# Layer 1: modulation steps between the projections, and the scaled triangles of four heads in one operation

## The chip, the cores and the metric

The kernel runs on one core of a Trainium2 chip. The metric is the device time of one execution in microseconds. A core has five engines with an instruction queue each: TensorE (PE; its weight loads are shown as PEld), VectorE (DVE), ScalarE (ACT), GpSimd (POOL) and SyncE (SP), which here only issues transfers of weights. Each works through its queue in order. Results of TensorE go to PSUM, everything else lies in SBUF.

## The reference, cut to what matters

The program is two networks of two layers each, behind one another, over 256 tokens of width 1024. The change lies in layer 1 of the first. That layer mixes tokens in two ways side by side, a state-space scan (`ssd`) and gated linear attention (`gla`), and six vectors made from `c`, the modulation, scale, shift and gate the layer's activations.

```
m_l = (jax.nn.silu(c) @ mod_w + mod_b)[:, None, :]
sh1_l, sc1_l, g1_l, sh2_l, sc2_l, g2_l = jnp.split(m_l, 6, axis=-1)
p_lat = _ada(x, norm1, sh1_l, sc1_l) @ w_in
...
x = x + g1_l * (o_l.astype(x.dtype) @ w_out)
x = x + g2_l * _sq_relu_mlp(_ada(x, norm2, sh2_l, sc2_l), mlp_w1, mlp_w2)
```

One chunk (128 tokens) of `ssd`, where `lac` is the logarithm of the decay per token and head:

```
cum = jnp.cumsum(lac, axis=1)
lmat = jnp.exp(jnp.where(lower, cum[:, :, None] - cum[:, None, :], -jnp.inf))
cb = jnp.einsum('bign,bjgn->bijg', cc, bc)
y = jnp.einsum('bijgr,bjgrp->bigrp', cb[..., None] * lmat, xdt)
y = y + jnp.einsum('bign,bgrpn->bigrp', cc, h) * jnp.exp(cum)[..., None]
```

## The kernel before, in words

Activations lie with the features on the partitions, 256 tokens of the context and 256 of the sequence in the columns. A large product is made with three matmuls of 32-bit numbers split in two parts: high by high, high by low, low by high (`mm3`, lines L219 to L221). Weights come as a stream of tiles `w` of 128x1024 numbers (0.524 MB), fetched on SP's queue into four buffers (L31). For a projection each half of a `w` is split: ScalarE casts it to `hi` (L44), VectorE subtracts to get `lo` (L45); there are four buffers of each. Once both halves are split, `w` is free. `gemm` makes one projection of 128 outputs from one `w`: 24 matmuls of 256 columns for one side, and 48 (from two fetches of the same weights) for context and sequence.

The modulation (`mod_steps`) needs no split: its tiles `w` are used as they are and become free when TensorE has read them. One step is two tiles with four matmuls of 32x256 each (L150; the trace shows every matmul of this number type as two):

```
        for u in range(16):
            k, o = u % 8, u // 8 * 256
            w = st.raw(16 * g + u)
            for j in range(4):
                nc.tensor.matmul(ps[32 * j : 32 * j + 32, o : o + 256], lhsT=self.cs[:, k, :], rhs=w[:, 256 * j : 256 * j + 256], start=(k == 0), stop=(k == 7))
            if u % 2:
                yield
```

Eight steps make a third of the modulation; layer 1 makes two thirds here, 16 steps, 32 tiles. The results are needed in the output projection and behind it.

PSUM has eight banks: two with the tag `mm` (for projections), two `sc`, four `po`.

The part of `layer1` around the change runs so in the program's text: projections for `gla`; `gla`'s levels (lines L1021 to L1109, many short operations on VectorE, ScalarE and GpSimd with short matmuls into `po`); eight projections (0 to 7) each followed by a convolution (`conv`, four operations L850 on VectorE) and a silu; the output of `gla` (L1129 to L1132); eight more projections `z` and `gs` (24 matmuls each); `ssd`. The first eight are six with 48 matmuls and two with 24. `ssd` first makes states in four rounds (transposes L915 and L927, products L933), then outputs: for two chunks, two directions and two groups of four heads a tile `lt` (a triangle of ones, a head's column of `la` as its scale), two matmuls with it (L975, L977), two exponentials, the products `MT` on GpSimd (L980) and `CE` on VectorE (L981), then the output matmuls (L989, L990). Behind it come the output projection, whose first half needs only `gla`'s result (96 matmuls from tiles `o4` to `o7`), and the memory block.

A scheduler turns this text into the queues: it puts ready work of lower rank where an engine would wait by its own estimate, so rows of several parts are mixed; text that stands earlier has the higher rank. Buffers go out in the order in which transfers and tiles are asked for.

Of the kernel before, what the change touches and what calls it, by code (L numbers as in the profile page):

```python
# [14 lines left out]
ALU = mybir.AluOpType  # L15
AX = mybir.AxisListType
PSUM = bass.MemoryType.PSUM
P = 128
# [57 lines left out]
class Kern:  # L76
# [825 lines left out]
    def ssd(self, pool, xs, bm, cm, z, d4, la, wend, etot, c1, out):  # L902
        nc = self.nc
        tri = lambda n: c1[:, COFF1[n][0] : COFF1[n][0] + COFF1[n][1]]
        TRI, ST = [tri("le"), tri("ge")], [tri("gt"), tri("lt")]
# [6 lines left out]
        for t in range(4):  # L912
# [17 lines left out]
            for d, w in xw.items():  # L930
# [9 lines left out]
                elif t == 1:  # L940
                    h = g(f"H{d}", (P, 8, 64))
# [7 lines left out]
                else:  # L949
                    h = hold[d]  # L950
# [5 lines left out]
        for c in range(2):  # L956
            ps = self.psum("sc")
            for gr in range(2):
                nc.tensor.matmul(ps[:, 128 * gr : 128 * gr + 128], lhsT=bm[gr][:, 256 + 128 * c : 384 + 128 * c],
                                 rhs=cm[gr][:, 128 * c : 128 * c + 128], start=True, stop=True)  # L960
            pair = []
            for d in range(2):
                cb = g("cb", (P, 2, 128), 2)
                nc.vector.tensor_tensor(cb, ps[:, 0:256].rearrange("p (g i) -> p g i", g=2),
                                        TRI[d].unsqueeze(1).broadcast_to([P, 2, 128]), op=ALU.mult)
                MT, CE = g("MT", (P, 8, 128), 2), g("CE", (P, 8, 128), 2)
                pair.append((MT, CE))
                for gr in range(2):
                    hs = slice(4 * gr, 4 * gr + 4)
                    lt = g("lt", (P, 4, 128), 2)  # L970
                    for h in range(4):
                        nc.vector.tensor_scalar(lt[:, h, :], TRI[d], la[:, 2 + c, 8 * d + 4 * gr + h : 8 * d + 4 * gr + h + 1], None, op0=ALU.mult)
                    l2 = lt.rearrange("p h i -> p (h i)")
                    p1 = self.psum("sc")
                    nc.tensor.matmul(p1, lhsT=ST[d], rhs=l2, start=True, stop=True)  # L975
                    p2 = self.psum("sc")
                    nc.tensor.matmul(p2, lhsT=self.C("ones"), rhs=l2, start=True, stop=True)  # L977
                    nc.scalar.activation(MT[:, hs, :], p1.rearrange("p (h i) -> p h i", h=4), AF.Exp)
                    nc.scalar.activation(CE[:, hs, :], p2.rearrange("p (h i) -> p h i", h=4), AF.Exp)
                    nc.gpsimd.tensor_tensor(MT[:, hs, :], MT[:, hs, :], cb[:, gr, :].unsqueeze(1).broadcast_to([P, 4, 128]), op=ALU.mult)  # L980
                    nc.vector.tensor_tensor(CE[:, hs, :], CE[:, hs, :],  # L981
                                            cm[gr][:, 128 * c : 128 * c + 128].unsqueeze(1).broadcast_to([P, 4, 128]), op=ALU.mult)
            for q in range(4):
                po = self.psum("po")
                for h in range(2):
                    o = po[64 * h : 64 * h + 64, 0:128]
                    hh = 2 * q + h
                    for d in range(2):
                        nc.tensor.matmul(o, lhsT=xd[d][c][:, hh, :], rhs=pair[d][0][:, hh, :], start=(d == 0), stop=False)  # L989
                        nc.tensor.matmul(o, lhsT=H[d][c][:, hh, :], rhs=pair[d][1][:, hh, :], start=False, stop=(d == 1))  # L990
                cs = slice(128 * c, 128 * c + 128)
                nc.vector.scalar_tensor_tensor(yt[q][:, cs], xs[q][:, 256 + 128 * c : 384 + 128 * c], self.V("d_skip")[:, q : q + 1], po[:, 0:128],
                                               op0=ALU.mult, op1=ALU.add)
# [140 lines left out]
    def layer1(self, xc, xl, sm, hm, HL):  # L1134

        tc, nc, a = self.tc, self.nc, self.a
# [10 lines left out]
        h = []  # L1147
# [56 lines left out]
        cp = pool("cv", C, "right")  # L1204
        cw, cb = [self.small(self.V(n), ALU.mult, 0.5, tag=n, pool=cp) for n in ("conv_w", "conv_b")]

        def silu(t, last):

            u = cp.tile([P, 512], F32, tag="th", name="th")[:, : t.shape[-1]]
            i = nc.scalar.activation(u, t, AF.Tanh)  # L1210
            self.issue(i, last)
            nc.vector.scalar_tensor_tensor(t, u, 1.0, t, op0=ALU.add, op1=ALU.mult)
            return i

        tanh, mods = [], (x for i in (1, 2) for x in self.mod_steps(1, i, cp, "mm"))
        for i in range(8):
            t = (xs + bm + cm)[i]
            self.conv(cp, self.gemm(st, 72 + 8 * i, *(h if i < 6 else h[1:])), i, t, cw, cb)
            if i == 0:
                for _ in mods:  # L1220
                    pass
            tanh.append(silu(t, last))
        for _ in mods:
            pass
        self.table(tanh)
        for _ in gla:
            pass
        last = self.last
        for i in range(8):
            nc.scalar.mul((z + gs)[i], self.gemm(st, 136 + 8 * i, h[1]), 0.5)  # L1230
        M.close()
        G.close()
        H.close()
        with ExitStack() as B:
            ssd = self.ssd(pool("ssd", B), xs, bm, cm, z, *dts, c1, o[:4])
            next(ssd)
            self.table([silu(t, last) for t in z + gs])
            for _ in ssd:
                pass
# [5 lines left out]
        with ExitStack() as B:  # L1245
            op = pool("os1", B, "right")
            self.w_out(1, [self.split(op, o[i], 256, f"o{i}") for i in range(4, 8)], xl, 0, None, st, 0)
            kv, *_ = self.memory(0, kvp, pool("mem", B, "right"))
        with ExitStack() as B:
            op = pool("os1", B)  # L1250
            HL = ExitStack()
            HL.enter_context(C)
            h, sm, step = self.mlp_enter(1, pool("mh1", HL, "right"), 0)
# [565 lines left out]
```

## Time and profile before

| | us |
|---|---|
| three runs, median | 2041.4 (2037.19 to 2044.7) |
| the profiled execution | 2037.99 |
| its span, first to last instruction | 2036.2 |
| TensorE, VectorE, ScalarE, GpSimd busy | 1914.3, 1417.9, 1160.3, 276.1 |

The profiled execution is one of the program's executions; 1.8 us of its time lie outside the span. All times in microseconds that are given as places, like 1077, count from the span's start. Busy times are sums over an engine's instructions without overlap; the ends of matmuls are modelled, so two matmuls that follow each other in 0.118 us are each shown with about 0.28.

### The profile page before, as it was taken

To read this page: it belongs to the slowest core of one execution; us is meant where nothing else is said; L and a number is where in the kernel's file an instruction comes from. 1 tells how busy PE (TensorE), PEld (TensorE's weight loads), DVE (VectorE), ACT (ScalarE), POOL (GpSimd) and SP (SyncE) were. 2 spreads that over 40 slices of the span, in tenths; PEclk is the share of its full clock that TensorE was granted. 3 is DMA by queue.
4 is the path that set the end of the run, shared out by engine and by line. 5 is a ranking of instruction groups with operands and counts; after the bars stand their busy time and mean duration, and the time that the engine had idled before them with its cause. 6 is when DMAs were issued, how large, how long until landed. Compare 5 with 4: busy or idle time off the path is not lost.

```text
span 2036.2 us, 42319 instructions
## 1 busy us (share of the span) xinstructions
PE 1914.3 (94%) x16330; PEld 1727.5 (85%) x16330; DVE 1417.9 (70%) x2962; ACT 1160.3 (57%) x2527; POOL 276.1 (14%) x407
## 2 busy tenths in 40 slices
PE   5999999889999999999979999999999999989997
PEld 2986668669889998899739779999889998889997
DVE  3775876589767685567588977567776656677664
ACT  3554563465545675566546658476565555565553
POOL 1421110230100000001230210000012201012210
PEclk8999999889999999999989999999999999999999
DMA  8432530624115555765376435555325554324553
GB/s 289 167 134 70 186 125 22 207 94 156 43 38 185 186 194 186 240 215 175 119 237 193 133 108 180 184 187 192 109 84 183 181 186 136 104 83 165 181 183 114
DMA packets 91785, 313.26 MB, mean 154 GB/s; under 512 B 10304, under 2 KB 17728, under 8 KB 91584
## 3 DMA queue, kind: packets, MB, share of 16 engines
q1 hardware_dynamic: 83376, 299.94, 44.5%
q10 hardware_dynamic: 8208, 10.63, 1.6%
q8 instruction: 128, 2.10, 0.4%
q14 instruction: 73, 0.60, 0.1%
HBM read 309.48 MB, written 1.05 MB: 153 GB/s over the span
## 4 chain that ended last, share of the span: by engine, by line
PE 74%; DVE 11%; DMA 5%; ACT 5%; issue 3%; POOL 2%; ACTq 0%; POOLq 0%; DVEq 0%; SPq 0%
PE mm L220 16%; PE mm L219 16%; PE mm L221 16%; PE po L220 3%; PE po L221 3%; PE po L219 3%; DMA w<-in_mlp 2%; DVE lo L45 2%; DMA w<-in_mod 2%; PE sc L528 1%; DMA w<-in_w_in 1%; PE po L1380 1%; PE mm L150 1%; ACT hi L44 1%; PE po L1443 1%
## 5 line engine op out<-in xcount | busy, mean ns | idle before, releaser
L45 DVE TENSOR_TENSOR lo<-w,hi 128x512 fp32r<-128x512 f32 x948 | 653.1, 696 | 276.2 <-ACT hi L44 255.7
L44 ACT CAST hi<-w 128x512 fp32r<-128x512 f32 x948 | 576.5, 618 | 428.4 <-PE mm L220 298.3
L219 PE MATMUL mm<-u_h,hi 128*128 128x256 f32 x1120 | 318.1, 284 | 4.4 <-ACT u_h L212 4.1
L221 PE MATMUL mm<-u_h,lo 128*128 128x256 f32 x1120 | 317.3, 284 | 0.0
L220 PE MATMUL mm<-u_l,hi 128*128 128x256 f32 x1120 | 316.9, 283 | 0.1
L219 PEld LDWEIGHTS mm<-u_h,hi 128*128 128x128 f32 x1120 | 213.7, 191 | 7.2 <-ACT u_h L212 4.7
L220 PEld LDWEIGHTS mm<-u_l,hi 128*128 128x128 f32 x1120 | 213.9, 191 | 0.9 <-DVE u_l L213 0.7
L221 PEld LDWEIGHTS mm<-u_h,lo 128*128 128x128 f32 x1120 | 213.5, 191 | 0.1
L150 PE MATMUL mm<-w,cs 128*32 128x256 f32 x640 | 69.3, 454 | 29.7 <-DMA w<-in_mod 29.3
L1585 POOL TENSOR_TENSOR ut<-ut,gt 128x256 f32<-128x256 f32 x44 | 53.4, 1214 | 200.7 <-ACT hi L44 170.5
L252 POOL TENSOR_SCALAR hf<-hf,g,mT 128x256 f32<-128x256 f32 x24 | 18.7, 779 | 413.0 <-ACT h1h L251 309.7
L150 PEld LDWEIGHTS mm<-w,cs 128*32 128x32 f32 x640 | 18.3, 117 | 59.8 <-DMA w<-in_mod 38.5
L213 DVE TENSOR_TENSOR u_l<-relu,u_h 128x256 fp32r<-128x256 f32 x96 | 40.7, 426 | 28.2 <-ACT u_h L212 28.0
L343 POOL TENSOR_SCALAR sht<-shf,mu 128x256 f32<-128x256 f32 x28 | 37.7, 1348 | 106.8 <-ACT shf L341 106.8
L212 ACT CAST u_h<-ut 128x256 fp32r<-128x256 f32 x44 | 17.9, 406 | 57.3 <-POOL ut L1585 57.3
L219 PE MATMUL mm<-h0h,hi 128*128 128x256 f32 x130 | 39.8, 309 | 9.7 <-ACT shf L341 4.9
L213 DVE TENSOR_TENSOR u_l<-ut,u_h 128x256 fp32r<-128x256 f32 x44 | 18.7, 425 | 42.7 <-ACT u_h L212 42.7
L1537 POOL TENSOR_TENSOR xl<-xl,yy 128x256 f32<-128x256 f32 x16 | 14.3, 891 | 228.5 <-DVE yy L1536 228.5
L221 PE MATMUL mm<-h0h,lo 128*128 128x256 f32 x130 | 38.8, 298 | 3.3 <-DVE lo L45 3.3
L821 ACT ACTIVATE relu<-relu 128x256 f32<-128x256 f32 x96 | 39.6, 416 | 3.8 <-DVE h7l L253 1.5
L68 POOL TENSOR_TENSOR sq<-sq 128x256 f32<-128x256 f32 x24 | 20.7, 864 | 154.6 <-ACT sq L60 151.7
L219 PEld LDWEIGHTS mm<-h0h,hi 128*128 128x128 f32 x130 | 24.8, 192 | 18.3 <-ACT shf L341 7.1
(1125 smaller groups left out, 6136.6 us busy)
## 6 DMA issues: line engine op xcount, KB each, us to landing
w<-in_mlp SPq DMA_DIRECT2D x192, 512.0 KB, 3.7
w<-in_w_in SPq DMA_DIRECT2D x102, 512.0 KB, 3.9
w<-in_mod SPq DMA_DIRECT2D x96, 512.0 KB, 5.5
w<-in_ffn_in SPq DMA_DIRECT2D x88, 512.0 KB, 3.8
w<-in_ffn_out SPq DMA_DIRECT2D x44, 512.0 KB, 4.0
w<-in_w_out SPq DMA_DIRECT2D x40, 512.0 KB, 3.8
w<-in_memkv SPq DMA_DIRECT2D x8, 512.0 KB, 3.8
xc<-in_ctxT ACTq DMA_DIRECT2D x16, 128.0 KB, 4.4
```

The lines of the kernel that those rows point to most:

```text
L44: nc.scalar.copy(self.hi, w)
L45: nc.vector.tensor_tensor(self.lo, w, self.hi, op=ALU.subtract)
L68: self.eng.tensor_tensor(sq, sq, self.acc, op=ALU.add)
L150: nc.tensor.matmul(ps[32 * j : 32 * j + 32, o : o + 256], lhsT=self.cs[:, k, :], rhs=w[:, 256 * j : 256 * j + 256], start=(k == 0), stop=( ...
L213: nc.vector.tensor_tensor(lo, src, hi, op=ALU.subtract)
L219: nc.tensor.matmul(out, lhsT=wh, rhs=xh, start=start, stop=False)
L220: nc.tensor.matmul(out, lhsT=wh, rhs=xl, start=False, stop=False)
L221: nc.tensor.matmul(out, lhsT=wl, rhs=xh, start=False, stop=stop)
L343: nc.gpsimd.tensor_scalar(t, f[:, 1:257], self.mu1[:, i : i + 1], None, op0=ALU.mult)
L528: nc.tensor.matmul(pz[h][:, :, p, :], lhsT=bk[s, p, :], rhs=rhs if c & 1 else rhs[:, ::-1, :], start=True, stop=True)
L821: nc.scalar.activation(r, r, AF.Square)
L1585: nc.gpsimd.tensor_tensor(w, w, t, op=ALU.mult)
```

## The change

The 16 steps of the modulation stood together behind projection 0, in a bank `mm`. Now one step stands behind each of the sixteen projections, in a bank `po`. The four operations that make `lt`, one for each head with the scale as a scalar operand, become one operation with two tensor operands, the triangle and the four scales, each read repeatedly.

```
-                    for h in range(4):
-                        nc.vector.tensor_scalar(lt[:, h, :], TRI[d], la[:, 2 + c, 8 * d + 4 * gr + h : 8 * d + 4 * gr + h + 1], None, op0=ALU.mult)
+                    nc.vector.tensor_tensor(lt, TRI[d].unsqueeze(1).broadcast_to([P, 4, 128]),
+                                            la[:, 2 + c, 8 * d + 4 * gr : 8 * d + 4 * gr + 4].unsqueeze(2).broadcast_to([P, 4, 128]), op=ALU.mult)
...
-        tanh, mods = [], (x for i in (1, 2) for x in self.mod_steps(1, i, cp, "mm"))
+        tanh, mods = [], (x for i in (1, 2) for x in self.mod_steps(1, i, cp, "po"))
         for i in range(8):
             t = (xs + bm + cm)[i]
             self.conv(cp, self.gemm(st, 72 + 8 * i, *(h if i < 6 else h[1:])), i, t, cw, cb)
-            if i == 0:
-                for _ in mods:
-                    pass
             tanh.append(silu(t, last))
-        for _ in mods:
-            pass
+            next(mods, None)
         self.table(tanh)
         for _ in gla:
             pass
         last = self.last
         for i in range(8):
             nc.scalar.mul((z + gs)[i], self.gemm(st, 136 + 8 * i, h[1]), 0.5)
+            next(mods, None)
+        for _ in mods:
+            pass
```

What this does to the queues, at three places. SP, from the end of layer 0's weights on (`in_mod` modulation, `in_w_in` projections of layer 1):

```order
 L31 DMA w<-in_mlp 128x1024 x21
 L31 DMA w<-in_w_in 128x1024 x14
-L31 DMA w<-in_mod 128x1024 x32
-L31 DMA w<-in_w_in 128x1024 x20
+L31 DMA w<-in_mod 128x1024 x2
+L31 DMA w<-in_w_in 128x1024 x2
+L31 DMA w<-in_mod 128x1024 x2
+L31 DMA w<-in_w_in 128x1024 x2
```

The two last rows go on to the end: two tiles of a step, then the next projection's two (one from projection 6 on), and the last step's two stand just ahead of `in_w_out`.

TensorE of the changed kernel where `gla`'s levels end (L1075, with `ql` and `kl`) and projection 2 begins (`h0h`):

```order
L1075 MATMUL po<-ql_12502,kl_12503 64x64
L892 MATMUL sc<-la,c_cst_9116 128x64 x2
L892 MATMUL sc<-la,c_cst_74 128x64
L150 MATMUL po<-w,cs 32x256 x16
L1129 MATMUL po<-qe_12562,S_12725 128x128
L1129 MATMUL po<-qe_12563,S_12943 128x128
L1130 MATMUL po<-at_12474,v 128x128
```

These 16 are the first two steps; no row of L150 stands ahead of them in layer 1's levels. Projections 0 and 1 stand ahead, mixed with the levels. In the kernel before, all 128 rows of L150 are mixed with the levels, and projection 1 comes behind the last of them.

TensorE of the changed kernel behind the last projection (its last step is the first row), up to `ssd`'s first matmul with `lt`; L933 is a product of the states:

```order
L150 MATMUL po<-w,cs 32x256 x8
L915 MATMUL sc<-c_cst_74,xs_9118 128x128
...
L927 MATMUL sc<-c_cst_74,bm_9123 128x128
L157 MATMUL po<-c_cst_74,modsb 128x128 x4
L933 MATMUL sc<-xw,bt 128x256 x2
...
L933 MATMUL sc<-xw,bt 128x256 x2
L959 MATMUL sc<-cm_9124,bm_9122 128x128
L959 MATMUL sc<-cm_9125,bm_9123 128x128
...
L975 MATMUL sc<-lt,c_cst_9116 128x512
```

These are the third and the fourth round of the states; the first two stand between the last projections. Nine matmuls of the output projection are among these rows, and two more before the end of `ssd`. Before, all four rounds stood behind the last projection, with 55 of the 96 matmuls between them and four more before the end.

## Rows read from the trace of the kernel before

**Rows 1.** The page: busy time of each engine, share, instructions.

```profile
PE 1914.3 (94%) x16330; PEld 1727.5 (85%) x16330; DVE 1417.9 (70%) x2962; ACT 1160.3 (57%) x2527; POOL 276.1 (14%) x407
```

**Rows 2.** Windows A to E: PE, PEld, DVE, ACT, POOL busy, PEclk, DMA share, GB/s.

```profile
1001.00:1077.00 76.00, 62.41 (x837) 32.88 (x835) 64.99 (x158) 39.93 (x122) 27.37 (x48) 0.89 0.63 213
1077.50:1140.50 63.00, 62.95 (x512) 61.28 (x511) 54.36 (x102) 47.10 (x93) 2.27 (x12) 1.00 0.58 181
1140.50:1159.40 18.90, 16.51 (x109) 14.25 (x107) 18.19 (x33) 11.46 (x24) 5.04 (x5) 1.00 0.26 84
1159.40:1188.70 29.30, 25.36 (x170) 14.91 (x168) 24.93 (x57) 13.55 (x26) 13.20 (x11) 1.00 0.14 46
1188.70:1195.30 6.60, 5.99 (x45) 5.49 (x43) 4.97 (x12) 3.29 (x9) 1.16 (x2) 1.00 0.37 129
```

**Rows 3.** DMA issues, 1001 to 1140: queue, KB each, median us to landing.

```profile
w<-in_mod SPq DMA_DIRECT2D x28, 512.0 KB, 5.6
w<-in_w_in SPq DMA_DIRECT2D x20, 512.0 KB, 4.2
```

**Rows 4.** Waits in stage A: who waited for whom, us, times, longest.

```profile
PE mm L150 <- DMA w<-in_mod: 8.0, 10, 1.8
DVE dt L882 <- PE sc L880: 2.4, 1, 2.4
DVE S L1109 <- PE sc L1103: 1.5, 2, 1.3
```

**Rows 5.** Timeline, PE: second and 24th matmul of a projection (start, us).

```profile
961.57 0.28 PE L220 MATMUL mm<-h0l,hi 128*128 128x256 f32 x1
...
964.16 0.28 PE L221 MATMUL mm<-h7h,lo 128*128 128x256 f32 x1
```

**Rows 6.** Timeline, PE, layer 0: steps (L150) and projections in turn.

```profile
377.75 1.07 PE L150 MATMUL mm<-w,cs 128*32 128x256 f32 x16
378.75 0.39 PE L219 MATMUL mm<-h0h,hi 128*128 128x256 f32 x1
...
381.82 1.07 PE L150 MATMUL mm<-w,cs 128*32 128x256 f32 x16
...
388.55 0.64 PE L150 MATMUL mm<-w,cs 128*32 128x256 f32 x8 [2.01 <-DMA w<-in_mod]
```

**Rows 7.** Timeline, DVE, stage B: convolution and `lo`.

```profile
1089.46 0.75 DVE L850 SCALAR_TENSOR_TENSOR xs<-cvf,conv_w,xs 128x512 f32<-128x512 f32 x1
1090.13 0.68 DVE L45 TENSOR_TENSOR lo<-w,hi 128x512 fp32r<-128x512 f32 x1
1090.73 0.74 DVE L850 SCALAR_TENSOR_TENSOR xs<-cvf,conv_w,xs 128x512 f32<-128x512 f32 x1
```

**Rows 8.** A window of layer 0, columns as in rows 2.

```profile
390.00:400.00 10.00, 7.80 (x39) 6.62 (x40) 4.82 (x12) 4.41 (x9) 1.46 (x2) 0.51 0.97 335
```

**Rows 9.** Groups by line and shape, ACT, 1078 to 1190: busy us, mean ns.

```profile
L44 ACT CAST hi<-w 128x512 fp32r<-128x512 f32 x48 | 29.0, 618 | 13.4 <-PE mm L220 13.3
```

**Rows 10.** Timeline of eight undisturbed `lt`; groups of DVE and POOL, 1140 to 1190.

```profile
1129.53 1.66 DVE L972 TENSOR_SCALAR lt<-c_cst,la 128x128 f32<-128x128 f32 x8
...
L972 DVE TENSOR_SCALAR lt<-c_cst,la 128x128 f32<-128x128 f32 x24 | 11.8, 542 | 1.0 <-PE sc L977 1.0
L981 DVE TENSOR_TENSOR CE<-CE,cm 128x512 f32<-128x512 f32 x8 | 5.7, 718 | 1.6 <-ACT CE L979 1.6
...
L980 POOL TENSOR_TENSOR MT<-MT,cb 128x512 f32<-128x512 f32 x8 | 11.4, 1429 | 20.4 <-ACT MT L978 20.4
```

**Rows 11.** Waits of PE in stage D.

```profile
PE sc L975 <- DVE lt L972: 3.0, 2, 1.7
PE po L990 <- DVE CE L981: 0.9, 1, 0.9
```

**Rows 12.** Timeline, PE, stage E: first and last of 37 output-projection matmuls.

```profile
1189.80 0.47 PE L221 MATMUL mm<-o7h,lo 128*128 128x256 f32 x1
...
1195.04 0.29 PE L221 MATMUL mm<-o7h,lo 128*128 128x256 f32 x1
```

## The prediction

> **What bounds the kernel now.** I read the page first: TensorE is busy 94% of the span [rows 1], so only stretches in which it stands still have something to give. I then cut layer 1 into five stages by what the trace shows at work, and asked for the busy time of each engine in each [rows 2]. Stage A (1001 to 1077 us) is the levels of `gla`; B (to 1140.5) the fifteen projections after the first; C (to 1159.4) the states of `ssd`; D (to 1188.7) its outputs; E (to 1195.3) what is left of the first half of the output projection, after which the memory block begins.
>
> The reader is to see three things in [rows 2]. In A VectorE works 65.0 of 76.0 us, and TensorE's 62.4 are short matmuls and the modulation: its 128 matmuls and 28 of its 32 transfers [rows 3] lie there, and the DMA engines are 63% busy. The steps do make TensorE wait for weights (8.0 us), and TensorE keeps VectorE waiting behind them 2.4 and 1.5 us [rows 4], but no more. In B TensorE is busy 62.95 of 63.0 us: it has no gap. In C, D and E it idles 2.4, 3.9 and 0.6 us. So B to E last 117.8 us and hold 110.8 us of TensorE's work.
>
> **What a step costs.** In a projection matmuls follow each other at (964.16 - 961.57) / 22 = 0.118 us [rows 5], so a 48-matmul projection is 5.66 us and a 24-matmul one 2.83. The same alternation as the change brings exists in layer 0: a step takes 378.75 - 377.75 = 1.0 us, and step and projection together 381.82 - 377.75 = 4.07 [rows 6]. The change adds no step, but 14 of the 16 move from A into B.
>
> **Term A.** The steps now accumulate in a `po` bank; `gla` needs all four, so by the order of the changed program the first two steps wait behind the last matmul of its levels. The four weight buffers meanwhile hold these steps' weights, and the weights of projection 2 can't be fetched. Only projection 1 comes into A. VectorE gets its four `lo` (0.60 us from start to start), four convolution steps (0.67) and one silu (as a `lo`, 0.60) [rows 7]: 2.4 + 2.7 + 0.6 = +5.7 us. The two waits on TensorE, 3.9 us, should go, since no transfer stands before those matmuls any more. A: +1.8. If all 11 us of VectorE's idle time went, A would be 65.0 + 5.7 = 70.7, or -5.3; if none, +5.7.
>
> **Term B.** TensorE's work: 63.0, less 5.7 for projection 1, plus 14.0 for the steps, plus the first half of the `ssd` states, which now stand between the last projections. C's 16.5 us of TensorE contain 55 matmuls of the output projection (96 in all, 37 left in E, 4 in D), 6.5 us; half of the other 10.0 is 5.0. Sum 76.3: B cannot be under +13.3 unless work moves on.
>
> The transfers are the second limit. After A 18 of `in_w_in` and 28 of `in_mod` are left, 46 of 0.524 MB, 24.1 MB; at the 335 GB/s of the fullest stretch [rows 8] that is 72 us. Two limits so close, coupled by four buffers, don't run at the larger one. For the ten 24-matmul projections: by the order on SP the weights of one are fetched when the step two periods earlier has released its buffer, so two periods hold one projection and one step (3.83), one landing (4.2 us for `in_w_in`, 5.6 for `in_mod` [rows 3]) and one cast of `hi` (0.62 [rows 9]): a period of 4.3 to 5.0, and I take the middle, 4.65. For the four 48-matmul ones TensorE needs 5.66 + 1.0 = 6.66 and four transfers 6.26 at 335 GB/s; I take 6.8. With the 6.4 us of B that are not projections (63.0 - 480 x 0.118) this is 46.5 + 27.2 + 6.4 = 80.1, and the 5.0 of `ssd` fit into the 8.2 us that the ten periods leave TensorE idle. B: +17.1. Ends: +13.3, and 10 x 5.0 + 4 x 7.7 + 6.4 + 5.0 = 92.2, or +29.
>
> **Term C.** Two of the four rounds of states are gone, and nearly all matmuls of the output projection between them (their weights now come after the last step's on SP): (18.9 - 6.5) / 2 = 6.2, and as the rounds wait for each other, 7: -11.9. Ends -14 (a round in 2.5) and -9.4 (half of 18.9).
>
> **Term D.** Four `lt` operations of 128x128 become one of 128x512. Undisturbed, eight take 1.66 us, 0.83 for four; beside GpSimd's `MT` product, which runs eight times 1.43 us, 24 take 542 ns each, 13.0 in all [rows 10]. The nearest row to the new form, the `CE` product of 128x512 with both inputs in SBUF, takes 718 ns among the same GpSimd work [rows 10]: six make 4.3. VectorE saves some 8 us, but the path only where TensorE waited: 3.0 for `lt` and 0.9 for `CE` [rows 11]; the rest of D is TensorE's own 25.4. D: -3.9. Ends: -3.9 and 0.
>
> The Trainium skill, SBUF — State Buffer, section Who interferes with whom, says that a VectorE instruction with two SBUF inputs contends with a GpSimd one that reads SBUF, and that the later one blocks for the whole of the other. By it the new `lt` is still held up, at most once for each, and D might give only about 2. The trace agrees that such forms are stretched: `CE` averages 718 ns.
>
> **Term E.** The changed order leaves 85 of the 96 output-projection matmuls for after D, 48 more than now. At 0.118 that is +5.7; at the pace of the 37 (1189.80 to 1195.04, 36 gaps, 0.146 each [rows 12]) +7.0. E: +6.
>
> **Sum.** 1.8 + 17.1 - 11.9 - 3.9 + 6 = +9.1 us. The profiled execution took 2037.99 us (span 2036.2 and 1.8 around it), so 2047.1 in its terms; it lies 3.4 below the median of the three runs, 2041.4. I give 2048.
>
> **The rivals.** *The transfers pace B and TensorE's clock falls.* In layer 0, as soon as the buffers that lay ready are used up, TensorE waits 2.01 us for one transfer [rows 6], and in the 10 us that follow its granted clock is 0.51, the 1.2 GHz level, with 335 GB/s flowing [rows 8]. At that clock a 24-matmul projection takes 2.83 / 0.51 = 5.5 and a period 7.5 instead of 4.65, +2.9. Three such periods make +9 more, about 2056; with B at its upper end, 2059 to 2064. Against it: B's own mean clock is 1.00, and TensorE would still be some 82% busy in each period. It decides from three periods on. The Trainium skill has the same mechanism in TensorE: Matmul & The Clock Gate, section HAM oscillation: waits for DMA let the array go cold. The row of layer 0 agrees.
>
> *The moved work is hidden anyway.* A shrinks to VectorE's 70.7 (-5.3) because no transfer blocks TensorE's queue there, and B to E hold only TensorE's work, 110.8 - 5.7 + 14.0 = 119.1 against 117.8 now (+1.3). That is the floor, -4.0: 2034. Half of the way up gives 2040. For it: the transfers at 335 GB/s need less than TensorE. Against it: B to E idle 7 us today, without such coupling.
>
> *Faster beyond that.* The floor of -4 is no half per cent, so it would take an effect that no row shows.
>
> **How the numbers follow.** A half per cent, 10 us, is about what a measurement of this kernel can tell from no change. The forecast (2041 to 2054) 0.57, of which 0.18 lies over 0.5%; the falling clock or a transfer-paced B (2055 to 2072) 0.22; hidden (2033 to 2041) 0.16; an unseen gain 0.05. So faster 0.05, within 0.39 + 0.16 = 0.55, slower 0.18 + 0.22 = 0.40. The range 2035 to 2064 leaves out the unseen gain, the last part of the hidden case and the third of the clock case that lies beyond 2064. With a sum so near a half per cent the side is open; the likelier is no change that can be measured.
>
> **What would show it.** In the profile after: A as long as now with TensorE mostly idle and the DMA engines quiet; then a stretch of about 80 us in which TensorE and DMA are both nearly full, with waits of L150 and of the casts on `in_mod` and `in_w_in`; `ssd`'s first transposes inside it; C of about 7 us; D of some 25 us with hardly a wait on `lt`; more matmuls of the output projection behind it. Wrong would be: A shorter by over 6 us, periods of 4 us or less or of 6 and more, a granted clock near 0.5 in B, or `lt` operations of over 1 us.

## The result and the profile after

The changed kernel takes 2072.2 us (median of four runs, 2057.7 to 2079.8) beside 2042.0 for the kernel before: 1.0129 times as long, with a 95% interval of 1.0096 to 1.0163. The forecast was 2048 with a range of 2035 to 2064. The profiled execution took 2074.46 us with a span of 2072.7, 36.5 more than before.

To see where, both traces are cut at the same six events: the first product of `gla`'s gates (L1021), the last operation of its levels (L1085), the last eviction of a projection `z` or `gs` (L1230 before, L1226 after), the first product with `lt` (L975), the last output product of `ssd` (L990) and the first product of the memory block. The borders differ by up to 2 us from those of [rows 2], and A begins 6 us earlier. The right column is a second profile of the same changed kernel (a run of 2064.4 us); the two differ by 6.6 us in B alone, so single profiles of B are read with that in mind.

| stage | before | forecast | after | second profile |
|---|---|---|---|---|
| A, levels of `gla` | 80.1 | +1.8 | 82.6 (+2.5) | 81.3 (+1.2) |
| B, projections | 66.4 | +17.1 | 105.1 (+38.7) | 98.5 (+32.1) |
| C, rest of the states | 17.7 | -11.9 | 8.9 (-8.8) | 8.9 (-8.8) |
| D, outputs of `ssd` | 29.2 | -3.9 | 26.6 (-2.6) | 26.6 (-2.6) |
| E, to the memory block | 6.6 | +6 | 12.1 (+5.5) | 12.1 (+5.5) |
| sum | 200.0 | +9.1 | 235.3 (+35.3) | 227.4 (+27.4) |

The page's row of busy times, against [rows 1]: no engine has more work to speak of.

```profile
PE 1927.4 (93%) x16330; PEld 1738.6 (84%) x16330; DVE 1418.0 (68%) x2938; ACT 1158.9 (56%) x2527; POOL 277.7 (13%) x407
```

The five stages of the kernel after, as in [rows 2] (PE, PEld, DVE, ACT, POOL busy, granted clock, DMA share, GB/s):

```profile
1000.80:1083.40 82.60, 58.07 (x660) 40.54 (x659) 73.63 (x167) 46.43 (x132) 28.15 (x50) 0.67 0.08 26
1083.40:1188.50 105.10, 92.00 (x729) 73.90 (x732) 61.26 (x110) 51.02 (x107) 6.10 (x14) 0.94 0.74 242
1188.50:1197.40 8.90, 6.44 (x53) 5.09 (x52) 7.50 (x17) 5.69 (x11) 1.61 (x2) 1.00 0.50 169
1197.40:1224.00 26.60, 25.03 (x167) 14.64 (x166) 20.96 (x28) 10.39 (x18) 13.11 (x11) 1.00 0.12 41
1224.00:1236.10 12.10, 11.56 (x92) 11.11 (x91) 10.29 (x22) 7.56 (x17) 1.21 (x2) 1.00 0.54 170
```

The reader is to see two things. In A the DMA engines, 63% busy before, now stand at 8%, and TensorE's clock is at 0.67 on average; all that was moved out of there now lies in B at 242 GB/s. And B, in which TensorE had no gap before, has 13 us without a matmul, with the clock at 0.94.

TensorE's waits in B of the kernel after (who waited for whom, us, times, longest):

```profile
PE mm L219 <- ACT hi L44: 9.1, 9, 3.1
PE po L150 <- DMA w<-in_mod: 3.4, 4, 1.5
PE mm L221 <- DVE lo L45: 0.4, 2, 0.2
```

and the landings of 1083 to 1188 us, against [rows 3] (KB each, median us from issue to landing):

```profile
w<-in_mod SPq DMA_DIRECT2D x27, 512.0 KB, 5.3
w<-in_w_in SPq DMA_DIRECT2D x16, 512.0 KB, 5.3
```

TensorE waits for the split of the projections' weights (`hi`), and the split for their landing or, in a stall that is shown further below, for its turn in ScalarE's queue.

**A measure for B.** The forecast went by the period of a step and a 24-matmul projection, from the first matmul of a projection to that of the next. The last ten projections give nine periods, and their mean is read so in every profile below. It was forecast as 4.65 us. What `gla` and `ssd` have between the projections is in the measured mean and was not in the 4.65. After, the mean is 7.26 (65.3 us from the first to the last), in the second profile 6.61, and in the kernel without the new `lt` 6.46.

### The profile page after: what moved, and what is told of

Read it like the earlier page. It is cut to its first block, busy times and chain, and to the rows that moved or that the text cites. A ratio compares the mean times of both kernels' runs of the same rounds, so it can differ in the third digit from the quotient of the medians.

```text
span 2072.7 us, 42274 instructions
## 1 busy us (share of the span) xinstructions
PE 1927.4 (93%) x16330; PEld 1738.6 (84%) x16330; DVE 1418.0 (68%) x2938; ACT 1158.9 (56%) x2527; POOL 277.7 (13%) x407
## 5 line engine op out<-in xcount | busy, mean ns | idle before, releaser
L221 PEld LDWEIGHTS mm<-u_h,lo 128*128 128x128 f32 x1120 | 213.1, 190 | 0.1
L252 POOL TENSOR_SCALAR hf<-hf,g,mT 128x256 f32<-128x256 f32 x24 | 18.8, 784 | 416.7 <-ACT h1h L251 353.3
L150 PE MATMUL mm<-w,cs 128*32 128x256 f32 x384 | 40.7, 470 | 23.1 <-DMA w<-in_mod 22.7
L213 DVE TENSOR_TENSOR u_l<-relu,u_h 128x256 fp32r<-128x256 f32 x96 | 40.7, 426 | 28.2 <-ACT u_h L212 27.9
L213 DVE TENSOR_TENSOR u_l<-ut,u_h 128x256 fp32r<-128x256 f32 x44 | 18.7, 425 | 43.8 <-ACT u_h L212 43.8
L150 PEld LDWEIGHTS mm<-w,cs 128*32 128x32 f32 x384 | 11.2, 121 | 43.9 <-DMA w<-in_mod 28.6
```

The costliest lines, as they stand in the source:

```text
L213: nc.vector.tensor_tensor(lo, src, hi, op=ALU.subtract)
L221: nc.tensor.matmul(out, lhsT=wl, rhs=xh, start=False, stop=stop)
```

## The experiments

### Each half of the change alone

First the kernel before with only the new `lt`, then the kernel after with only the old.

```
-                    for h in range(4):
-                        nc.vector.tensor_scalar(lt[:, h, :], TRI[d], la[:, 2 + c, 8 * d + 4 * gr + h : 8 * d + 4 * gr + h + 1], None, op0=ALU.mult)
+                    nc.vector.tensor_tensor(lt, TRI[d].unsqueeze(1).broadcast_to([P, 4, 128]),
+                                            la[:, 2 + c, 8 * d + 4 * gr : 8 * d + 4 * gr + 4].unsqueeze(2).broadcast_to([P, 4, 128]), op=ALU.mult)
```

> The kernel before with the new form of lt alone; the steps stay where they were. My theory puts the whole loss on the moved steps, and the four operations in one give what the changed kernel shows in stage D, some 2 us: 2039 to 2041, ratio 0.998 to 1.000. The rival, that the new form takes part in the loss (some of its eight operations took up to 1754 ns beside GpSimd, against 4 x 542 before, and 3 us of TensorE's waits on lt are at stake either way), expects 2043 or more.

Measured: 2040.7, ratio 1.0003 (0.9984 to 1.0022). D is 27.9 us in its profile, 1.3 less than before, but nothing of it can be measured in the whole.

> The changed kernel with the old form of lt: the moved steps alone. My theory expects the whole loss here and the gain of lt missing, 2073 to 2077. The rival, that the new lt has a part in the loss, expects less than 2070.

Measured: 2068.3, ratio 1.0128 (1.0101 to 1.0155). The moved steps are the whole loss. The time was given as 2073 or more and lies in the other theory's range, under 2070; but the ratio equals that of the changed kernel (1.0129), and the new `lt` alone changed nothing, so no part of the loss that can be measured is left for `lt`. This stage B, whose granted clock is 1.00, is nearly as long (97.8 us) as that of the second profile of the changed kernel (98.5, clock 0.95):

```profile
1081.10:1178.90 97.80, 88.16 (x732) 70.11 (x736) 61.78 (x118) 51.03 (x107) 5.50 (x13) 1.00 0.77 259
```

So a fallen clock in B isn't what makes it long.

### The steps without their transfers

```
-            w = st.raw(16 * g + u)
+            w = None if x else st.raw(16 * g + u)
...
+                rhs = x[k] if x else w[:, 256 * j : 256 * j + 256]
...
+        tanh, mods = [], (x for i in (1, 2) for x in self.mod_steps(1, i, cp, "po", xl))
```

> The changed kernel in which the 16 steps read the activations xl that lie in SBUF, 256 columns for every matmul, in place of fetched weights: the same 128 matmuls at the same places, but 32 transfers fewer, and their results are not the modulation. If the transfers pace stage B (46 at 2.3 us each), it shrinks from some 107 us to TensorE's own 76 to 82, and the time falls to 2040 to 2050 though TensorE's clock stays at 0.50 in stage A. If the fallen clock or TensorE's work at the new place costs the time, 2062 to 2072 stay.

Measured: 2053.4, ratio 1.0055 (1.0033 to 1.0076): between the two ranges that were given. Over half of the loss of 1.29% goes with the 32 transfers, 0.55% stays. Its stages A and B:

```profile
990.90:1075.10 84.20, 62.97 (x701) 45.22 (x704) 75.11 (x167) 49.39 (x136) 30.06 (x50) 0.72 0.08 26
1075.10:1149.70 74.60, 74.60 (x678) 61.67 (x670) 54.66 (x106) 48.50 (x103) 2.75 (x11) 1.00 0.44 141
```

B has no gap and is 8.2 us longer than before: that is TensorE's own price for work that it had done in A's free time. With no step's tile in the buffers, the weights of projection 2 come early too, so that a little more of the projections lies in A; the difference to the changed kernel holds this as well. Seven of the nine periods are 4.0 us; the two others, 14.0 and 5.1, hold the output of `gla` and the end of the first eight steps, and the mean of all is 5.26. So without the steps' transfers the nine take 47.3 us, against 65.3 and 59.5 in the two profiles of the changed kernel, which hold less of `gla` and, in place of it, states of `ssd`.

### Does the clock of stage A cost anything?

In A of the changed kernel the granted clock is at 0.50, the 1.2 GHz level, from 1031 to 1081. Two of its 10-us windows:

```profile
1051.00:1061.00 10.00, 5.86 (x98) 4.57 (x98) 8.75 (x22) 6.66 (x19) 3.99 (x8) 0.50 0.01 2
1061.00:1071.00 10.00, 1.54 (x30) 1.07 (x28) 9.27 (x26) 3.53 (x11) 1.84 (x5) 0.50 0.00 0
```

The next kernel has, beside all of the change, the 128 matmuls once more on data in SBUF where they stood before:

```
             self.conv(cp, self.gemm(st, 72 + 8 * i, *(h if i < 6 else h[1:])), i, t, cw, cb)
+            if i == 0:
+                for n in (1, 2):
+                    for _ in self.mod_steps(1, n, cp, "mm", xl):
+                        pass
```

> The changed kernel with the same 128 matmuls once more where the kernel before had its steps, on activations that lie in SBUF (nothing is fetched for them; what they write to the modulation is overwritten by the real steps): TensorE has in stage A the work that it had before, stage B is as in the changed kernel. If the fallen clock of stage A lengthens A and the start of B, the granted clock there returns to 0.9 or more, A falls by some 7 us, and the time to 2060 to 2066. If the clock there costs nothing, because VectorE sets A's length, A stays or grows by the added work, and the time is 2070 to 2076.

Measured: 2066.2, between the two ranges that were given; the ratio, 1.0125 (1.0095 to 1.0155), is that of the changed kernel. Its stages A and B:

```profile
995.80:1079.30 83.50, 72.80 (x929) 46.63 (x928) 74.12 (x173) 47.04 (x133) 27.77 (x48) 0.84 0.10 33
1079.30:1175.10 95.80, 85.70 (x723) 68.18 (x726) 61.66 (x112) 51.41 (x107) 6.20 (x16) 1.00 0.77 260
```

The clock rose to 0.84, less than expected, and A did not become shorter: VectorE works 74 of its 83 us either way. What a clock of 1.00 in A would do isn't shown. B keeps a period of 6.49.

### How many steps, in which bank, in how many buffers

With the steps in `mm` in place of `po`:

> The changed kernel with the steps in a bank mm in place of po, still one behind each projection: the first two steps need not wait for the end of gla's levels, so their buffers come free early and the weights of projection 2 are fetched in stage A. If the transfers held up behind the first two steps matter, 2055 to 2064. If the loss is the pace of 46 transfers in B as a whole, it stays at 2064 to 2075; and since a step's bank leaves the projections one bank mm, each then has to wait for the eviction of the one before, which can only add.

Measured: 2060.3, ratio 1.0098 (1.0076 to 1.0119). B is 89.9 us. The first steps now run in A (from 1014 us on), and the time lies where it was expected if what the first two steps hold up matters. By the ratios that is worth some 0.3%, less what the narrower `mm` costs, which is hardly clear of the noise; the rest of the loss stays.

With the first eight steps together as before, and eight between `z` and `gs`:

```
-        tanh, mods = [], (x for i in (1, 2) for x in self.mod_steps(1, i, cp, "po"))
+        tanh, mods = [], self.mod_steps(1, 2, cp, "po")
...
+            if i == 0:
+                self.mod(1, 1, cp, "mm")
```

> The changed kernel with the first eight steps together behind projection 0 in mm, as before, and only the other eight between the projections z and gs, in po. If the loss is in proportion to the transfers that are moved out of stage A, where the DMA engines now stand still, it halves: 2052 to 2060. If it comes from the coupling of a step with a 24-matmul projection (two tiles of a step to one of a projection in four buffers), eight of the ten such periods stay and most of the loss too: 2060 to 2068. If only the last few steps count, 2066 and more.

Measured: 2049.6, ratio 1.0039 (1.0014 to 1.0064), less than half of the loss: neither the proportion (2052 at the least) nor the coupling of eight periods (2060) is borne out by the time. The long periods are there in its profile (a run of 2057.4 us): the mean is 6.38.

Three buffers of `hi` and of `lo` in place of four, then the space so won as a fifth `w`:

```
-        self.pool, self.wb, self.hib = (pool, 2, 4) if pool else (K.wpool, 4, 4)
+        self.pool, self.wb, self.hib = (pool, 2, 4) if pool else (K.wpool, 5, 3)
```

> Control for the next: the changed kernel with three buffers of hi and of lo in place of four, in the whole program. The split runs less far ahead: 2066 to 2085 if four are little used, more where they are.

> The changed kernel with five weight buffers w and three of hi and of lo (the space of one goes to the other), to be read against the kernel with four and three. If stage B is long because a buffer comes free only when TensorE has run a step, and not because the DMA engines can do no more (225 to 235 GB/s in B against 335 in the fullest stretch), a fifth buffer lets each transfer start earlier: B falls by 10 us or more against the control. If the transfers themselves take 2.3 us each, B changes by less than 4 us.

Measured: 2085.4 (1.0193 to 1.0238) with four, 2068.8 (1.0121 to 1.0167) with five. The fifth buffer gives 16.6 us, but not where it was expected: B goes from 95.2 to 90.8, not by the 10 us that buffers coming free too late would have given, C from 9.5 to 11.6, and the mean period from 6.36 to 6.33. Of the 13.7 us between the two profiled spans 12.8 lie ahead of stage A, which begins at 1001.1 us with four and at 988.3 with five: it is work before this layer's `gla` that gains. TensorE's waits for `in_mod` (2.4 us with four) are gone with five, those for the weights' split are not (5.5 and 6.5).

### One transfer of a step for one of a projection

```
-            if u % 2:
+            if u % every == every - 1:
                 yield
...
+        tanh, mods = [], self.mod_steps(1, 2, cp, "po", 1)
```

> As many tiles moved as in the kernel that interleaves eight steps with z and gs (16 of 32), but one tile, half a step, behind each of the sixteen projections in place of two behind each of the last eight. My theory now: with two tiles of a step and one of a projection in a turn of four buffers, a step's second tile takes the buffer of the first one of the step before, so that one period holds a whole landing (5.2 us) and the read; with one and one, a tile takes the buffer of the tile two periods earlier, a period needs only half a landing, 2.7 us, less than TensorE's 3.3. So no wait of TensorE for in_mod behind gla's levels, stage B under 78 us (82.2 in the other kernel), and 2040 to 2047. If the number of transfers moved sets the loss, it is as in the other kernel: 2048 to 2054.

Measured: 2052.6, ratio 1.0048 (1.0023 to 1.0072). B is 75.4 us, TensorE waits 0.6 us in it and never for a transfer. First matmuls of half steps and projections, TensorE:

```profile
1143.35 0.64 PE L150 MATMUL po<-w,cs 128*32 128x256 f32 x8
1143.92 0.38 PE L219 MATMUL mm<-h0h,hi 128*128 128x256 f32 x1
1146.96 0.64 PE L150 MATMUL po<-w,cs 128*32 128x256 f32 x8
1147.53 0.39 PE L219 MATMUL mm<-h0h,hi 128*128 128x256 f32 x1
```

The period is 1147.53 - 1143.92 = 3.61 us, TensorE's own: 2.83, half a step, and 0.28 for the change of hands. Two transfers in a period are hidden, three are not. The time that was expected from it did not come: A to E together are 213.1 us, with two tiles to a projection for half the steps they were 213.7. Where TensorE has no wait, the states of `ssd` are not drawn into B (C is 18.7 us here, 9.0 there). So this kernel confirms the hidden transfers and not the gain. The theory it was built on, that a step's second tile sets the period, isn't confirmed by that: in the second profile of the changed kernel TensorE waited 0.2 us in B for `in_mod` and 6.1 for the casts of the projections' weights.

### Is it `gla`'s output between the projections?

In the two profiles of the changed kernel some periods take 7 to 10 us, and one stretch without a new transfer, 1131 to 1145 us, lies where `gla`'s output norm stands in the queues of ScalarE and VectorE. A second look at the same kernel:

> The changed kernel once more, for a second profile: if the stretch of 14.5 us in which no weights were fetched (1131 to 1145 us) is an accident of one execution, B is nearer to 96 us, as in the two kernels with the same stage B; if it belongs to the order of the queues, it comes again at the same place.

Measured: 2064.4 in one run; B 98.5. The stall came again at the same place with 9.6 us (1125.5 to 1135.2), so it belongs to the order and its size to the execution. Then `gla`'s output ahead of all, in the kernel after and in the kernel before:

```
+        for _ in gla:
+            pass
+        last = self.last
         tanh, mods = [], (x for i in (1, 2) for x in self.mod_steps(1, i, cp, "po"))
...
         self.table(tanh)
-        for _ in gla:
-            pass
-        last = self.last
```

> The changed kernel with the output of gla (its products, norm and scaling) in the program's text ahead of projection 0's convolution and of the steps, so that these rows stand in the queues right behind the levels and not between the projections. In the changed kernel's two profiles three or four of the ten 24-matmul periods take 7 to 10 us, and they lie where gla's output norm stands in the queues of ScalarE and VectorE ahead of the splits of the weights. If that collision makes the long periods, they go: B shrinks by 8 us or more, 2054 to 2062. If every period is long because of the transfers and the buffers alone, B shrinks by less than 4, 2064 to 2072.

> The same reordering in the kernel before, whose projections run at 2.8 us a piece with TensorE full: there is no stall to remove, only two loads of ScalarE's table less. It should stay within 4 us of the kernel before, 2038 to 2046; should it gain more, it is a version that beats both.

Measured: 2078.7, ratio 1.0172 (1.0148 to 1.0195), and 2052.0, ratio 1.0045 (1.0028 to 1.0062). Both are slower, against every number given, and B of the first is 114.5 us. The output block by itself now takes 13.6 us at half the clock, with nothing else at work, and that hides what the periods do:

```profile
1078.00:1091.60 13.60, 13.60 (x42) 9.67 (x42) 1.90 (x6) 4.08 (x11) 0.00 (x0) 0.50 0.00 0
```

Behind it the nine periods have nothing of `gla` among them. None takes over 7.5 us, so the longest ones were `gla`'s; but the mean is still 6.46. Here is the one with the longest landing (issues of SP, casts of ScalarE, first matmuls of projections):

```profile
1161.15 0.37 SPq L31 DMA_DIRECT2D w<-in_w_in  x1
1162.51 1.14 ACT L44 CAST hi<-w 128x512 fp32r<-128x512 f32 x2 [1.54 <-DMA w<-in_w_in]
...
1163.17 0.38 PE L219 MATMUL mm<-h0h,hi 128*128 128x256 f32 x1 [1.28 <-ACT hi L44]
1164.48 3.73 SPq L31 DMA_DIRECT2D w<-in_mod  x2
1168.67 0.33 SPq L31 DMA_DIRECT2D w<-in_w_in  x1
1169.20 1.14 ACT L44 CAST hi<-w 128x512 fp32r<-128x512 f32 x2 [1.53 <-DMA w<-in_w_in]
...
1169.87 0.39 PE L219 MATMUL mm<-h0h,hi 128*128 128x256 f32 x1 [1.26 <-ACT hi L44]
```

The weights issued at 1161.15 are cast at 1169.20, 8.05 us later, the moment they land; the first matmul follows at 1169.87. Over the nine periods the weights take 6.4 us to land on average.

### Half the bytes

Each of a step's transfers brings 128x512, and its matmuls read that twice:

```
-            w = st.raw(16 * g + u)
+            n = 2 if l and g else 4
+            w = st.raw(16 * g + u, 256 * n)
...
+                c = 256 * (j % n)
```

> The changed kernel in which a step's transfer brings half a tile (128x512, 0.262 MB) and its four matmuls read those 512 columns twice: the same 46 transfers, buffers and matmuls in the same order, 7.3 MB fewer behind gla's levels; the results of the steps are not the modulation. If the long periods come from the transfers sharing the DMA engines (a tile of weights lands in 5.3 to 6.6 us among them, 4.0 without), the landing of in_w_in falls to 4.0 to 4.6, the mean period of the ten from 6.5 to 7.0 to 5.2 or less, B by 10 us or more, and the time to 2048 to 2058. If it is the order of four buffers alone, each period with a whole latency whatever the size, B changes by less than 5: 2063 to 2070.

Measured: 2069.4, ratio 1.0144 (1.0115 to 1.0173), no gain, as the order of buffers alone would have it. Landings fell to 4.7 us for `in_w_in` and 3.8 for `in_mod`, TensorE's waits in B from the 7.4 us of the second profile of the changed kernel to 3.5, and B to 92.5; but C is 15.8, the rest of the states having been put there, and the mean period is 6.27, with `gla`'s output in the long ones. That leaves open which of the two counts, so both at once:

> gla's output ahead of the interleaving and half a tile for each of a step's transfers, both at once (what the steps compute is not the modulation). The block of gla's output costs about 13 us at its new place, so this is read by the ten periods, not by the time. If the growing landing (6.6 us with full tiles and nothing of gla between) makes a period of 6.5, half tiles bring it to 5.2 or less, the projections' weights from issue to first matmul from 7.3 to 5.5 us, and the time to 2064 or less. If a period is as long whatever the bytes, it stays at 6 and more, and the time over 2072.

Measured: 2077.3, ratio 1.0160 (1.0128 to 1.0193). The time lies over 2072, where it was given for a period that does not depend on the bytes. The periods, by which this was to be read, say otherwise: their mean is 5.40 us, between the 5.2 and the 6 that were given and nearer to the first, against 6.46 with full tiles, and B is 102.4 against 114.5 us. The landings of B:

```profile
w<-in_w_in SPq DMA_DIRECT2D x18, 512.0 KB, 4.5
w<-in_mod SPq DMA_DIRECT2D x28, 256.0 KB, 3.9
```

and the pair of rows to compare with those above:

```profile
1154.36 0.37 SPq L31 DMA_DIRECT2D w<-in_w_in  x1
...
1158.52 1.14 ACT L44 CAST hi<-w 128x512 fp32r<-128x512 f32 x2
...
1159.80 0.47 PE L221 MATMUL mm<-h0h,hi 128*128 128x256 f32 x1
```

5.44 us from issue to first matmul in place of 8.72; over the nine periods the mean is 5.6 in place of 7.5. So the landing of the weights, grown by the transfers that flow beside them, is a part of the period. What that is worth in time isn't shown: of the 12 us that B won C gives back 7, 13.0 us against 5.7, since fewer states stand in B, and 2077.3 and 2078.7 can't be told apart.

### A version to beat both

The kernel before with the new `lt` and two `z` projections ahead of the steps:

```
+                for j in range(2):
+                    nc.scalar.mul((z + gs)[j], self.gemm(st, 136 + 8 * j, h[1]), 0.5)
                 for _ in mods:
                     pass
```

> A version that could beat both: the kernel before with the new lt, and the projections z0 and z1 ahead of the 16 steps, which stay together in mm. Stage A has idle TensorE time and idle DMA time at its start, and a z projection costs VectorE only its two lo (1.2 us), no convolution. If A's TensorE time is there to take, two projections leave B (-5.7 us) and A grows by at most 2.4: 2037 to 2041, ratio 0.998 to 1.000. The rival: the steps' transfers start two weights later, and what of the steps doesn't fit into A any more stands in B with its transfers, 2042 to 2050.

Measured: 2053.2, ratio 1.0058 (1.0030 to 1.0085). That is slower than either range that was given. In its profile (a run of 2071.3 us, the slowest of twelve) the rival's mechanism is there: the steps run from 1034 to 1118 us, 25 us past the end of A. No kernel of these is faster than the kernel before.

## Why the prediction was wrong, by its steps

**What bounds the kernel** stands. A is VectorE's (73.6 us of 82.6 now), B was TensorE's.

**Term A**, +1.8, measured +2.5 and +1.2: right, also in its parts. VectorE has 73.6 us of work in A where the same cut gives 68.6 before, +5.0 for the +5.7 forecast, and less idle time. That the clock stood at 0.50 for 50 us didn't show in A.

**Term B is the step that failed**, and in it the period: "a period of 4.3 to 5.0, and I take the middle, 4.65". It measured 7.3 and 6.6; 6 and more had been named as a sign of being wrong. B is 22 and 15 us longer than forecast. The nine periods take 23 and 18 us more than nine of 4.65; some 6 and 4.5 of that are products of `gla` that the forecast had counted apart, so 17 and 13 are the period's. Another 5 are the four projections of 48 matmuls, forecast as 6.8 each, measured as 8.2 and 8.0.

The order of the chain is right: two periods hold a projection, a step, a landing and a cast, and in all nine of both profiles it was a step's matmul (L150) that released the buffer of the weights. Its terms were too small. Each of the nine chains, from the first matmul of a projection to that of the second one after it, averaged (us; the last two columns are the kernels with `gla`'s output ahead of all, the last with half the bytes):

| part of the chain | forecast | after | second profile | `gla` first | and half bytes |
|---|---|---|---|---|---|
| first matmul to issue of the weights | 3.83 | 6.3 | 6.0 | 5.2 | 5.1 |
| landing of the weights | 4.2 to 5.6 | 5.9 | 5.5 | 6.4 | 4.5 |
| landed to first matmul | 0.62 | 2.2 | 1.6 | 1.1 | 1.1 |
| two periods | 8.7 to 10.1 | 14.4 | 13.1 | 12.7 | 10.7 |

The largest miss is the first part, +2.5 and +2.2: it was put in as the bare 3.83 of a projection and a step, with nothing for the products of `ssd` and `gla` that run between them, for a step that waits, or for the change of hands. The landing misses 4.9, the middle of its two values, by 1.0 and 0.6. The 4.2 was that of the kernel before, whose DMA engines in B were 58% busy [rows 2]; with the steps' tiles flowing beside them single ones took up to 9 us. With `gla`'s output ahead of all the two parts miss alike, by 1.4 and 1.5, and half the bytes take 1.9 off the landing and 2.0 off the sum. That shows the landing to be one of the terms that were too small; how the first part divides among what stands in it was not measured. In the second profile of the changed kernel, the two steps, the issue between them, and the projection:

```profile
1152.97 1.07 PE L150 MATMUL po<-w,cs 128*32 128x256 f32 x16
...
1154.11 0.37 SPq L31 DMA_DIRECT2D w<-in_w_in  x1
...
1158.00 1.38 PE L150 MATMUL po<-w,cs 128*32 128x256 f32 x16
...
1159.98 1.14 ACT L44 CAST hi<-w 128x512 fp32r<-128x512 f32 x2 [1.04 <-DMA w<-in_w_in]
...
1160.65 0.38 PE L219 MATMUL mm<-h0h,hi 128*128 128x256 f32 x1 [0.57 <-ACT hi L44]
```

The step at 1152.97 frees the buffer, the weights are issued at 1154.11 and used at 1160.65: 6.54 us where 4.8 to 6.2 had been allowed. With the 3.83 of a projection and a step, half the sum is 5.2, and with a few of `ssd`'s and `gla`'s matmuls between, one arrives at the periods of 5.0 to 6.5 that five of the nine have. The longer ones come where `gla`'s output is in the queues. The longest stall of the first profile (SP, then ScalarE and VectorE):

```profile
1130.73 0.33 SPq L31 DMA_DIRECT2D w<-in_w_in  x1
1133.70 10.32 SPq L31 DMA_DIRECT2D w<-in_mod  x2
1145.28 0.33 SPq L31 DMA_DIRECT2D w<-in_w_in  x1
...
1138.01 0.38 ACT L200 ACTIVATE sq<-po 128x256 f32<-128x256 f32 x1 [3.88 <-PE po L1130]
1138.71 1.28 ACT L173 ACT_TABLE_LOAD   x1
1141.74 1.13 ACT L44 CAST hi<-w 128x512 fp32r<-128x512 f32 x2
...
1142.38 1.29 DVE L45 TENSOR_TENSOR lo<-w,hi 128x512 fp32r<-128x512 f32 x2
1143.59 0.16 DVE L159 TENSOR_TENSOR mT<-po,c_vecs 128x8 f32<-128x8 f32 x1
```

The weights asked for at 1130.73 landed at 1135.96, but their cast began only at 1141.74: ahead of it ScalarE's queue had the norm of `gla`'s output (L200, L173), which waited for a product of `gla`. Their buffer came free with the second `lo`, at 1143.67, and SP issued its next transfer at 1143.70. The profile puts this wait of SP, 7.8 us, down to `mT` (L159), which ended after that issue and so can't have released it. From 1130.73 to 1145.28 no weights were asked for, and I had no term for that.

Nor had I one for the change of hands between a step and a projection, 0.28 us a time in the kernel with half steps; the row of layer 0 showed it (4.07 for what adds up to 3.83 [rows 6]), and I used the 3.83.

**Term C**, -11.9, measured -8.8; **term E**, +6, measured +5.5: right in kind, C 3 us short.

**Term D**, -3.9, measured -2.6, of which -1.3 in the kernel with the new `lt` alone. The waits of TensorE went as forecast, from 3.0 [rows 11] to 0.3:

```profile
PE po L990 <- DVE CE L981: 1.1, 1, 1.1
PE sc L975 <- DVE lt L971: 0.3, 1, 0.3
```

But the operation is dearer than the `CE` row promised (least, median and longest ns of eight):

```profile
L971 DVE TENSOR_TENSOR lt<-c_cst,la x8: 678/998/1754, 1147.4 to 1216.0; 128x512 f32<-128x512 f32 x8
```

Single ones of over 1 us were named as a sign against the forecast, and they are there. Nor was the 718 ns a sign of much stretching: in the kernel before seven of the eight `CE` took 675 to 680 ns and one 1003. In the changed kernel `CE` is dearer too, 1.14 us on average, so that `lt` and `CE` cost VectorE 16.9 us in D where they had cost 18.8: 2 us saved, not the 8 of the forecast. The path hardly felt it, since VectorE's queue had room. The Trainium skill, SBUF — State Buffer, section Who interferes with whom, has such a form held up while GpSimd reads; the spread from 678 to 1754 ns agrees, though no run here took GpSimd's work away.

**The rivals.** The first had two halves. The transfers do take part in pacing B, and they do it without a fallen clock: in the kernel with the moved steps alone B's granted clock is 1.00. In the changed kernel it is 0.94 and 0.95, but with the same loss, so it isn't what makes the loss; TensorE is busy 92.0 and 90.8 us in B there and 88.2 at 1.00, so the clock's share is some 3 to 4 us by that, an estimate. The Trainium skill, TensorE: Matmul & The Clock Gate, section HAM oscillation, describes waits for DMA as what lets the clock fall; here the clock of B is 0.94 and 0.95 in profiles in which TensorE waited 12.9 and 7.4 us in it, and 1.00 in the kernel with the moved steps alone, in which it waited 9.6. The hidden case was wrong: what made TensorE wait in A before (8.0 us for `in_mod` [rows 4]) had not been on A's path, and the same transfers are on B's.

**The split.** By the kernel without transfers, 0.55% of the 1.29% stays without them. In its profile A is 4.1 us longer than before, B 8.2 longer and the rest 2.8 shorter, so this is in the main TensorE's work that left A's free time. The other 0.74%, or 15 us, goes with the transfers: landings, stalls, the clock, and weights of projection 2 that come too late for A. These four were not each measured alone. Open too is where the kernel with half steps loses its half per cent: its B is 9.0 us longer than before, of which 14 half steps (+7.0), projection 1 (-5.65) and 14 changes of hands (+3.9) explain 5.3.

## What to carry to other kernels

A block of transfers that stands in a stretch bound by another engine can already be hidden, as it was here; spread among work whose own weights come through the same buffers and queue, two tiles to one, it was not. A period's landing time is to be taken at the load that the change makes, not at the load before: here three transfers in a period made 4.2 us into 5.3 and more, two in a period cost TensorE no wait. The time that an engine needs from one turn to the next is to be taken with all that the order puts between, not as the bare sum of two parts: that was the larger miss. A releaser that ends after what it is said to release is the wrong one; look for what ended just ahead. And when a wait goes, look what the scheduler had put into it: twice B became shorter by 6 to 12 us here and C longer by about 7.

## What was unexpected of the hardware

Half the bytes in a step's transfer took its landing from 5.4 to 3.9 us and that of the full tiles beside it from 5.7 to 4.5 (the two kernels with `gla`'s output first). TensorE's granted clock stood at 0.50 for 50 us in which its queue held little but `gla`'s short matmuls; adding the 128 matmuls back raised the mean of the stage only from 0.67 to 0.84.
